# Casts of the gated heads held in order on ScalarE, their projection one gate later, and eight conv taps moved to an earlier product, in a hybrid mixer block

## The chip, the cores and the metric

The kernel runs on one core of one Trainium2 chip. Its time is the device time of one execution in microseconds (us). The kernel before takes 981.49 us, the median of three runs (981.21 to 982.88).

The core's engines each take instructions from a queue of their own, in order, and wait on semaphores for one another: TensorE (PE: matmuls, with its weight loads shown as PEld), VectorE (DVE), ScalarE (ACT), GpSimd (POOL) and SyncE (SP), which here only issues transfers.

## The reference

One layer on x of 512 positions by 1024 channels. Its first part, which the change touches, is cut to this:

```python
hn = rms_norm(h, g_mix_pre)
z_sgu, z_conv, z_pool, z_gate = split(hn @ w_in)         # 2048, 2048, 1024, 3072 columns
# A: spatial gating
u, v = split(gelu(z_sgu))
v = layer_norm(v, g_v, b_v)                              # in 4 blocks of 128 positions, 8 heads of 128 channels
mixed = einsum('hij,bnjhc->bnihc', masked(w_s), v) + b_s
br_a = (u * mixed) @ w_sgu_out
# B: conformer convolution
a, gate = split(z_conv)
c = causal_depthwise_conv(a * sigmoid(gate), w_dw) + b_dw # 31 taps in each channel
br_b = silu(layer_norm(c, g_ln, b_ln)) @ w_conv_out
# C: pooling: trailing means over 2, 4, 8, 16 positions in 4 groups of 256 channels, minus z
br_c = (einsum('bsgc,gcd->bsgd', trailing_means(z_pool) - z_pool, w_pool) * s_pool) @ w_pool_out
g = sigmoid(z_gate)                                      # three gates of 1024 channels
merged = g[0] * br_a + g[1] * br_b + g[2] * br_c
h = h + rms_norm(merged @ w_out, g_mix_post)
```

A SwiGLU part with 2816 channels and a gated embedding follow; the change leaves their code as it is.

## The kernel before

**Products.** Activations stand transposed, 128 channels by 512 positions a tile, 8 tiles. Every float32 operand is held as two parts in TensorE's float32r format: `hi`, the value cast, and `lo`, the rest. A product of two 128-blocks is three matmuls (`mm3`): hi by hi, hi by lo, lo by hi. An output tile of 128 channels from 1024 inputs is 24 matmuls. The weights of one such tile are one block `raw` of 128x1024, loaded by SP; ScalarE casts `hi<-raw` and VectorE subtracts `lo<-raw,hi`. Three buffers of each rotate, so a cast waits until TensorE has finished with an older block, and a load until VectorE has finished with an older `raw`.

**Stages around the change, in the program's order.** Conv input (`ps_ag`, a and gate of branch B). v's product (`ps_nat`, positions on the partitions; `natural`), gelu, and v's normalisation (`v_norm`, `v_gain`: rows `v_all`). u's product, also `ps_nat`. Between its pieces stand the heads: `mix_head(h)` splits v of head h (`v_split`), multiplies it by the head's 128x128 matrix (`ps_mix`), gates it with u (`gated`), turns its 32x32 blocks (`corners`) and sends it by way of DRAM (`home`) back into `sgu`, turned as a whole. `split_head(h)` then casts the head that has come back (ACT `sgu<-sgu`) and subtracts (DVE `sgu<-sgu`). Then the eight gate tiles of branch A (`ps_gate`, a sigmoid into `merged`) and the eight tiles of its projection (`ps_br<-sgu`), which start `SGU_LAG` gates behind. Then the pooling input (`ps_z`, copied to `z_all`): for each of four groups of two tiles, GpSimd adds up the windows (`win`), VectorE finishes them with three instructions on `win`, ScalarE casts `pl_hi<-win`, VectorE subtracts `pl_lo<-win,pl_hi`, and TensorE maps the group (`ps_pool`, 24 matmuls), called map 1 to 4 here. Then the gates of branch C with its projection (`ps_br<-pool`), branch B's norm, gates and projection, and the rest.

**Conv taps.** The 31 taps of each of the 8 conv tiles are VectorE work for which no other engine waits until branch B's norm: one `TENSOR_SCALAR` and thirty `SCALAR_TENSOR_TENSOR acc<-h_conv,vec,acc` a tile. They stand in the list `background`; `drain(n)` places n of them. `TAPS` says how many go behind each tile of the conv input, each weight block of v's product, each gate or projection tile of branch A, each tile of the pooling input, and each tile of branch C's gates and projection; `TAPS_U` does so for u's product.

**What sets the order.** The program is recorded in the order of the code, and a scheduler then places each engine's instructions by its own estimate of when their inputs are ready. Only where `order` is on (`InOrder`) does an instruction stay behind everything that was recorded before it on its engine. On before's ScalarE the casts of the heads are placed freely; `gated` and `corners` on VectorE and all conv taps are held.

Of the kernel before, what the change touches and what calls it, by code (L numbers as in the profile page):

```python
# [7 lines left out]
F32 = mybir.dt.float32  # L8
# [4 lines left out]
ALU = mybir.AluOpType  # L13
# [30 lines left out]

N_WARM = 8

TAPS = (4, 3, 5, 4, 5)
TAPS_U = 4


# [42 lines left out]
def hybrid_block(  # L93
# [8 lines left out]
    order = InOrder(tc)  # L102
    dve, act_e = order.engine(nc.vector), order.engine(nc.scalar)
# [21 lines left out]
    def t2(name, n=T):  # L125
        return tmp.tile([P, n], F32, tag="t2", name=name)
# [50 lines left out]
    def split(hi, lo, src):  # L177
        act_e.copy(hi, src)
        dve.tensor_tensor(out=lo, in0=src, in1=hi, op=ALU.subtract)
# [75 lines left out]
    def drain(n):  # L255
        for _ in range(min(n, len(background))):
            with order():
                background.pop(0)()
# [63 lines left out]
    def add_mix(*blocks):  # L322
        for b in blocks:
            weights.add(w_mix[b])
# [3 lines left out]
    add_mix(*range(C_V, C_V + 8))  # L328
    weights.add(w_sgu, "tm")
    add_mix(*range(C_U, C_U + 8))  # L330
    SGU_LAG = 5
    for n in range(KT + SGU_LAG):
        if n < KT:
            add_mix(C_M + n)
        if n >= SGU_LAG:
            add_mix(S_SGU + n - SGU_LAG)
    for g in GROUPS:
# [96 lines left out]
    def glu(k, ps_a, ps_g, scale=None):  # L434
        sig = t2("sig")
        src = ps_g
        if scale is not None:
            dve.tensor_tensor(out=sig, in0=ps_g, in1=scale, op=ALU.mult)
            src = sig
        act_e.activation(out=sig, in_=src, func=AF.Sigmoid)  # L440
        if scale is not None:
            dve.tensor_tensor(out=sig, in0=sig, in1=scale, op=ALU.mult)
        dve.tensor_tensor(out=h_of(k), in0=ps_a, in1=sig, op=ALU.mult)
        queue_conv(k)
# [14 lines left out]
    with order():  # L459
        (c0, c1), cut = first_cuts(0)  # L460
        hi, lo = (w[:, c0:c1] for w in first[0])
# [4 lines left out]
        hi, lo = (w[:, slice(*cut)] for w in first[0])  # L466
# [40 lines left out]
        for i in range(KT):  # L507
            t = t2("nrm")
            dve.scalar_tensor_tensor(out=t, in0=x_all[:, i], scalar=col("g_mix_pre", i),
                                     in1=x_inv, op0=ALU.mult, op1=ALU.mult)  # L510
            act_e.copy(hn[i][:, 0], t)
            if low:
                low()
            low = lambda i=i, t=t: dve.tensor_tensor(out=hn[i][:, 1], in0=t, in1=hn[i][:, 0],
                                                     op=ALU.subtract)
# [6 lines left out]
    for k in range(N_RAW, KT):  # L522
        pair = []
        for _ in range(2):
# [4 lines left out]
            pair.append(ps)  # L529
            drain(TAPS[0])  # L530
        glu(k, *pair)


    def natural(dst, evacuate, taps):


        for c in range(2):
            banks = [bank("ps_nat") for _ in range(NB)]
            for kk in range(4):
                hi, lo = weights.get()  # L540
                for b in range(NB):
                    if b == NB // 2:
                        yield c, kk, 0
                    ts = slice(b * P, (b + 1) * P)
                    for j in range(2):
                        k = 2 * kk + j
                        a = hn[k]
                        ws = slice(j * T, (j + 1) * T)
                        pe.matmul(banks[b], lhsT=a[:, 0, ts], rhs=hi[:, ws],
                                         start=k == 0, stop=False)  # L550
                        pe.matmul(banks[b], lhsT=a[:, 1, ts], rhs=hi[:, ws],
                                         start=False, stop=False)
                        pe.matmul(banks[b], lhsT=a[:, 0, ts], rhs=lo[:, ws],
                                         start=False, stop=k == KT - 1)
                drain(taps)
                if kk == 3:
                    for b in range(NB):
                        evacuate(dst, b, c, banks[b])
                yield c, kk, 1
# [23 lines left out]
    nc.sync.dma_start(out=b_bc, in_=gb_v[1:2, :].broadcast_to([P, D]))  # L583
    for _ in natural(v_all, v_gelu, TAPS[1]):
        pass
# [32 lines left out]
    def mix_head(h):  # L618
        cs = slice(h * P, (h + 1) * P)
        vs = slot("tm", "v_split")  # L620
        split(vs[:, 0], vs[:, 1], of_head(v_tile, h))
        ps = bank("ps_mix")
        mm3(ps, sg_hi[:, cs], sg_lo[:, cs], vs[:, 0], vs[:, 1], True, True)


        gated, corners = t2("gated"), t2("corners")
        sgu_T[h] = slot("br", f"sgu{h}")
        with order():
            dve.scalar_tensor_tensor(out=gated, in0=ps, scalar=col("b_sgu_s", h),
                                     in1=of_head(u_tile, h), op0=ALU.add, op1=ALU.mult)  # L630
            dve.transpose(out=corners, in_=gated)
        home = dram.tile([P, T], F32, name="home")
        for i in range(NQ):
            nc.sync.dma_start(
                out=home[:, i * P:(i + 1) * P].rearrange("(q a) f -> a q f", q=NQ),
                in_=corners[i * Q:(i + 1) * Q].rearrange("a (q f) -> a q f", q=NQ))
        nc.sync.dma_start(out=sgu_T[h][:, 1].bitcast(F32), in_=home)

    def split_head(h):
        hi, lo = sgu_T[h][:, 0], sgu_T[h][:, 1]  # L640
        split(hi, lo, lo.bitcast(F32))


    heads = {(1, 0): ((), (0,)), (1, 1): ((), (1,)), (2, 1): ((0,), (2,)),
             (3, 0): ((1,), ()), (3, 1): ((), (3,))}
    for c, kk, behind in natural(u_all, u_gelu, 0):
        pe_order.on = c == 1 or kk == 3
        done, mixed = heads.get((kk, behind), ((), ())) if c == 1 else ((), ())
        for h in done:
            split_head(h)  # L650
        for h in mixed:
            mix_head(h)
        if behind:
            drain(TAPS_U)
# [5 lines left out]
    def gate_tile(dst, taps, between=None):  # L660
        ps = bank("ps_gate")
        w = weights.get()
        half = KT // 2 if between else KT
        product(ps, w, hn[:half], last=not between)
        if between:
            between()
            product(ps, [h[:, half * P:] for h in w], hn[half:], k0=half)
        act_e.activation(out=dst, in_=ps, func=AF.Sigmoid)
        drain(taps)

    def branch_tile(acts, taps):
        ps = bank("ps_br")
        product(ps, weights.get(), acts)
        drain(taps)
        return ps

    for n in range(KT + SGU_LAG):
        if n < KT:
            gate_tile(merged[:, n, :], TAPS[2])
        if n < SGU_LAG:  # L680
            for h in ((2,), (3,), (4,), (5, 6), (7,))[n]:
                split_head(h)
            for h in ((4,), (5, 6), (7,), (), ())[n]:
                mix_head(h)
        else:
            i = n - SGU_LAG
            ps = branch_tile(sgu_T, TAPS[2])

            gate = merged[:, i, :].rearrange("p (n i b) -> p i n b", n=NB, i=NQ)
            dve.tensor_tensor(out=gate, in0=ps.rearrange("p (i n b) -> p i n b", n=NB, i=NQ),  # L690
                              in1=gate, op=ALU.mult)
# [6 lines left out]
    def pool_windows(gi):  # L698
        w = WINDOWS[gi]
        z = z_all[:, 2 * gi:2 * gi + 2, :]  # L700
        cur, d = z, 1
        while d < w:
            nxt = slot("tm", "win", F32)
            nc.gpsimd.tensor_tensor(out=nxt[:, :, d:], in0=cur[:, :, d:], in1=cur[:, :, :T - d], op=ALU.add)
            nc.gpsimd.tensor_copy(nxt[:, :, :d], cur[:, :, :d])
            cur, d = nxt, 2 * d
        head = rcnt[:, None, :w].broadcast_to([P, 2, w])
        dve.tensor_tensor(out=cur[:, :, :w], in0=cur[:, :, :w], in1=head, op=ALU.mult)
        dve.tensor_tensor(out=cur[:, :, :w], in0=cur[:, :, :w], in1=z[:, :, :w], op=ALU.subtract)
        dve.scalar_tensor_tensor(out=cur[:, :, w:], in0=cur[:, :, w:], scalar=1.0 / w,  # L710
                                       in1=z[:, :, w:], op0=ALU.mult, op1=ALU.subtract)
        hi = slot("tm", "pl_hi")
        lo = slot("tm", "pl_lo")
        split(hi, lo, cur)
        pooled[gi] = hi, lo
# [13 lines left out]
    for g in GROUPS:  # L729
        for n in (2 * g, 2 * g + 1):  # L730
            ps = bank("ps_z")
            product(ps, weights.get(), hn)
            act_e.copy(z_all[:, n, :], ps)
            drain(TAPS[3])
        pool_windows(g)
# [5 lines left out]
    for n in range(KT + POOL_LAG):  # L741
        if n < KT:
            gates.append(t2("gate"))
            gate_tile(gates[n], TAPS[4], maps.get(n))
        if n == KT + POOL_LAG - 1:
# [104 lines left out]
    with order():  # L850
# [6 lines left out]
        for i in range(N_HALF):  # L857
            n = KT - N_HALF + i
# [9 lines left out]
        for i in range(N_HALF):  # L868
            n = KT - N_HALF + i
# [232 lines left out]
```

## Time and profile before

| | |
|---|---|
| median of 3 runs | 981.49 us |
| profiled execution, its own time | 981.05 us |
| its span, first to last instruction | 979.1 us |
| PE busy | 967.0 us (99%) |
| DVE busy | 679.1 us (69%) |
| ACT busy | 349.0 us (36%) |
| POOL busy | 70.8 us (7%) |
| mean granted TensorE clock | 0.996 of full speed |

The span is what the trace holds; 1.95 us of the profiled execution's own time lie around it, and the median of the runs is 0.44 us above that execution. In a row of a timeline stand the start, the duration, the engine, the operation and its tiles (out<-in), and in brackets the engine's idle time just before it with what ended that. "xN" is a number of instructions that the row merges. A matmul's duration overlaps the next one's, so TensorE's pace is read from starts. In the waits stand the total, the number of times, and the longest.

### The profile page before, as it was taken

Reading aid. Unit: us, or ns where it says so; the run is one execution under the profiler, and the core shown is the slowest. Engines: PE = TensorE matmul, PEld = TensorE weight load, DVE = VectorE, ACT = ScalarE, POOL = GpSimd, SP = SyncE. Lnnn points to the kernel's source line nnn. Section 1 sums busy time; section 2 is a strip of 40 time slices with the busy share of each in tenths; the row PEclk is TensorE's granted clock in tenths of the full one; section 3 lists DMA queues with packets and bytes.
Section 4 is the critical chain, followed back from the end, with each engine's and each line's share of the span. In section 5 each row is a group of like instructions: output and inputs, shape, how many; then the busy total and the mean of one; then the engine's idle time right before and its main releaser. Section 6 shows DMA issues by size and latency. Waiting matters only on the chain.

```text
span 979.1 us, 11157 instructions
## 1 busy us (share of the span) xinstructions
PE 967.0 (99%) x4397; PEld 803.4 (82%) x4397; DVE 679.1 (69%) x876; ACT 349.0 (36%) x467; POOL 70.8 (7%) x49
## 2 busy tenths in 40 slices
PE   9999999999997999999999999999999999999998
PEld 6888888888886878888888998888888888888887
DVE  7987789989999899977655688454445442223684
ACT  7522324333223332246525443332323232223451
POOL 0100013000022712220000000000000000000000
PEclk9999999999998999999999999999999999999999
DMA  8723322553322233232337303223232223334311
GB/s 301 203 88 106 109 87 81 164 160 112 108 78 84 76 108 108 87 108 86 108 108 237 107 1 128 87 86 104 90 108 87 99 83 100 100 100 140 110 65 65
DMA packets 36484, 106.92 MB, mean 109 GB/s; under 512 B 4176, under 2 KB 8784, under 8 KB 36432
## 3 DMA queue, kind: packets, MB, share of 16 engines
q1 hardware_dynamic: 35568, 103.95, 32.0%
q0 software_dynamic: 720, 2.23, 1.3%
q8 instruction: 34, 0.56, 0.2%
q14 instruction: 18, 0.15, 0.0%
q10 hardware_dynamic: 144, 0.04, 0.0%
HBM read 99.78 MB, written 4.19 MB: 106 GB/s over the span
## 4 chain that ended last, share of the span: by engine, by line
PE 79%; DVE 15%; issue 3%; DMA 2%; ACT 0%; SPq 0%; DVEq 0%; ACTq 0%
PE ps_f L80 25%; PE ps_fo L80 12%; PE ps_br L80 9%; PE ps_gate L80 8%; DVE acc L80 8%; PE ps_ag L80 6%; PE ps_o L80 5%; PE ps_pg L80 4%; PE ps_nat L80 4%; DVE lo L80 4%; PE ps_first L80 3%; PE ps_ple L80 1%; DMA sgu<-home 1%; DVE v_all L80 1%; DMA home<-corners 1%
## 5 line engine op out<-in xcount | busy, mean ns | idle before, releaser
L80 ACT CAST hi<-raw 128x1024 fp32r<-128x1024 f32 (+2 forms) x160 | 164.8, 1031 | 420.6 <-PE ps_br L80 85.4
L80 DVE TENSOR_TENSOR lo<-raw,hi 128x1024 fp32r<-128x1024 f32 (+2 forms) x158 | 205.6, 1302 | 104.6 <-ACT hi L80 103.8
L80 DVE SCALAR_TENSOR_TENSOR acc<-h_conv,vec,acc 128x509 f32<-128x509 f32 (+14 forms) x240 | 188.5, 790 | 4.3
L80 PE MATMUL ps_f<-hg,hi 128*128 128x512 f32 (+1 forms) x608 | 183.3, 383 | 0.0
L80 PEld LDWEIGHTS ps_f<-hg,hi 128*128 128x128 f32 x608 | 113.1, 188 | 22.5
L80 PE MATMUL ps_gate<-hn,hi 128*128 128x512 f32 x384 | 119.0, 389 | 0.0
L80 PE MATMUL ps_f<-hg,lo 128*128 128x512 f32 (+1 forms) x304 | 116.4, 383 | 0.0
L80 PE MATMUL ps_fo<-f,hi 128*128 128x512 f32 x352 | 108.4, 389 | 0.0
L80 PEld LDWEIGHTS ps_gate<-hn,hi 128*128 128x128 f32 x384 | 72.1, 188 | 15.0
L80 PE MATMUL ps_nat<-hi,hn 128*128 128x512 f32 x256 | 78.8, 389 | 0.0
L80 PEld LDWEIGHTS ps_fo<-f,hi 128*128 128x128 f32 x352 | 66.1, 188 | 13.6
L80 PE MATMUL ps_gate<-hn,lo 128*128 128x512 f32 x192 | 74.8, 390 | 1.2 <-DVE lo L80 1.2
L80 PE MATMUL ps_fo<-f,lo 128*128 128x512 f32 x176 | 68.5, 389 | 0.0
L80 PEld LDWEIGHTS ps_f<-hg,lo 128*128 128x128 f32 x304 | 57.1, 188 | 11.1
L80 DVE TENSOR_TENSOR f<-ps_f,h_inv 128x512 f32<-128x512 f32 x22 | 15.2, 690 | 59.4 <-PE ps_f L80 59.4
L80 PEld LDWEIGHTS ps_nat<-hi,hn 128*128 128x128 f32 x256 | 48.1, 188 | 9.9
L80 PE MATMUL ps_nat<-lo,hn 128*128 128x512 f32 x128 | 49.8, 389 | 0.0
L80 PE MATMUL ps_ag<-hn,hi 128*128 128x512 f32 x160 | 49.3, 389 | 0.0
L80 PEld LDWEIGHTS ps_gate<-hn,lo 128*128 128x128 f32 x192 | 36.0, 188 | 9.2 <-DVE lo L80 1.7
L80 PE MATMUL ps_z<-hn,hi 128*128 128x512 f32 x128 | 41.6, 406 | 0.0
L80 DVE TENSOR_TENSOR silu<-ps_f,h_inv 128x512 f32<-128x512 f32 x22 | 15.2, 690 | 36.7 <-PE ps_f L80 36.6
L80 PE MATMUL ps_br<-sgu,hi 128*128 128x512 f32 x128 | 39.4, 389 | 0.0
(220 smaller groups left out, 1488.6 us busy)
## 6 DMA issues: line engine op xcount, KB each, us to landing
raw<-in_w_mix SPq DMA_DIRECT2D x90, 512.0 KB, 3.2
raw<-in_w_ffn_in SPq DMA_DIRECT2D x44, 512.0 KB, 3.2
raw<-in_w_ffn_out SPq DMA_DIRECT2D x16, 448.0 KB, 3.3
raw<-in_w_ffn_out SPq DMA_DIRECT2D x8, 512.0 KB, 3.5
raw<-in_w_ple_gate SPq DMA_DIRECT2D x8, 512.0 KB, 3.5
x_all<-in_xT SPq DMA_DIRECT2D x8, 256.0 KB, 6.0
home<-corners SPq DMA_DIRECT2D x32, 64.0 KB, 2.6
sgu<-home SPq DMA_DIRECT2D x8, 256.0 KB, 2.6
```

The lines of the kernel that those rows point to most:

```text
L80: inst = op(*args, **kw)
```

## The change

The casts of the eight returned heads (`act_e.copy(hi, ...)` in `split_head`) are recorded under `order`, so that each stays behind all that was recorded before it on ScalarE; the calls are placed later (heads 0 and 1 in the fourth weight block of u's second half, heads 2 to 7 one gate later than before), and the projection starts six gates behind (`SGU_LAG`), with the order of its weight blocks changed to match. Behind each of the eight weight blocks of v's product stand four conv taps where there were three, and behind each of the eight tiles of the pooling input three where there were four.

```diff
-TAPS = (4, 3, 5, 4, 5)
+TAPS = (4, 4, 5, 3, 5)
...
-    SGU_LAG = 5
+    SGU_LAG = 6
...
     def split_head(h):
         hi, lo = sgu_T[h][:, 0], sgu_T[h][:, 1]
-        split(hi, lo, lo.bitcast(F32))
+        with order():
+            act_e.copy(hi, lo.bitcast(F32))
+        dve.tensor_tensor(out=lo, in0=lo.bitcast(F32), in1=hi, op=ALU.subtract)
...
-    heads = {(1, 0): ((), (0,)), (1, 1): ((), (1,)), (2, 1): ((0,), (2,)),
-             (3, 0): ((1,), ()), (3, 1): ((), (3,))}
+    heads = {(1, 0): ((), (0,)), (1, 1): ((), (1,)), (2, 1): ((), (2,)),
+             (3, 0): ((0,), ()), (3, 1): ((1,), (3,))}
...
-            for h in ((2,), (3,), (4,), (5, 6), (7,))[n]:
+            for h in ((), (2,), (3,), (4,), (5, 6), (7,))[n]:
                 split_head(h)
-            for h in ((4,), (5, 6), (7,), (), ())[n]:
+            for h in ((4,), (5, 6), (7,), (), (), ())[n]:
                 mix_head(h)
```

The order that the scheduler makes of it differs on every engine from v's product to branch C's gates, with the same instructions in all. Three places follow.

ScalarE, from just ahead of head 0's cast, before; `sgu_` with a number is one returned head's tile, the lowest number is head 0:

```order
L80 CAST v_split<-v_all 128x512
L80 CAST sgu_1350<-sgu_1350 128x512
L80 CAST hi<-raw 128x1024
L80 CAST v_split<-v_all 128x512
L80 ACTIVATE u_all<-ps_nat 128x16x32
L80 CAST sgu_1380<-sgu_1380 128x512
L80 ACTIVATE u_all<-ps_nat 128x16x32 x2
L80 CAST hi<-raw 128x1024
L80 ACTIVATE u_all<-ps_nat 128x16x32
L80 CAST v_split<-v_all 128x512
L80 CAST sgu_1434<-sgu_1434 128x512
L80 CAST hi<-raw 128x1024
```

ScalarE now, again from just ahead of head 0's cast, to the first gate's sigmoid (`merged`):

```order
L80 CAST hi<-raw 128x1024
L80 CAST sgu_1358<-sgu_1358 128x512
L80 CAST v_split<-v_all 128x512
L80 ACTIVATE u_all<-ps_nat 128x16x32 x3
L80 CAST hi<-raw 128x1024
L80 ACTIVATE u_all<-ps_nat 128x16x32
L80 CAST sgu_1388<-sgu_1388 128x512
L80 CAST v_split<-v_all 128x512
L80 CAST hi<-raw 128x1024
L80 ACT_TABLE_LOAD
L80 ACTIVATE merged<-ps_gate 128x512
```

Heads 0 and 1 are cast one weight block (`hi<-raw`) later than before; head 2, which stands in the first list, is beyond the end of the second, two blocks later and behind two sigmoids.

VectorE, from the subtraction of a map's weights to the last window row of map 2 (`win<-win,z_all 128x2x4`), before; `acc` rows are conv taps:

```order
L80 TENSOR_TENSOR lo<-raw,hi 128x512
L80 SCALAR_TENSOR_TENSOR acc_154<-h_conv_150,vec,acc_154 128x488
L80 SCALAR_TENSOR_TENSOR pool_2373<-ps_pool,vec,pool_2373 128x512
L80 SCALAR_TENSOR_TENSOR win<-win,z_all 128x2x508
L80 TENSOR_TENSOR win<-win,rcnt 128x2x4
L80 SCALAR_TENSOR_TENSOR acc_154<-h_conv_150,vec,acc_154 128x487
L80 TENSOR_TENSOR lo<-raw,hi 128x1024
L80 TENSOR_TENSOR win<-win,z_all 128x2x4
```

The same stretch of VectorE now:

```order
L80 TENSOR_TENSOR lo<-raw,hi 128x512
L80 SCALAR_TENSOR_TENSOR acc_154<-h_conv_150,vec,acc_154 128x484
L80 SCALAR_TENSOR_TENSOR win<-win,z_all 128x2x508
L80 TENSOR_TENSOR win<-win,rcnt 128x2x4
L80 SCALAR_TENSOR_TENSOR pool_2377<-ps_pool,vec,pool_2377 128x512
L80 SCALAR_TENSOR_TENSOR acc_154<-h_conv_150,vec,acc_154 128x483
L80 TENSOR_TENSOR win<-win,z_all 128x2x4
```

The 128x1024 weight subtraction has moved behind the last window row, and the tap at the same place is four taps further in its tile (483 elements left where 487 were).

TensorE at map 4, the difference from before to now (the first two matmuls of the map take `pl_hi`, its other ten begin with `pl_lo`):

```order
+L80 MATMUL ps_pool<-pl_hi,hi 128x512 x2
 L80 MATMUL ps_gate<-hn_160,hi 128x512 x2
 L80 MATMUL ps_gate<-hn_160,lo 128x512
-L80 MATMUL ps_gate<-hn_161,hi 128x512
-L80 MATMUL ps_pool<-pl_hi,hi 128x512 x2
-L80 MATMUL ps_gate<-hn_161,hi 128x512
-L80 MATMUL ps_gate<-hn_161,lo 128x512
-L80 MATMUL ps_gate<-hn_162,hi 128x512 x2
-L80 MATMUL ps_gate<-hn_162,lo 128x512
-L80 MATMUL ps_gate<-hn_163,hi 128x512
 L80 MATMUL ps_pool<-pl_lo,hi 128x512
```

The first two matmuls of map 4 stand four matmuls earlier in TensorE's queue, and the other ten follow three matmuls behind them instead of six.

## The prediction

> **What bounds the kernel now.** I read the page first, then TensorE's waits, then its timeline at each of them, and last the queue of the engine it waited for.
>
> ```profile
> PE 967.0 (99%) x4397; PEld 803.4 (82%) x4397; DVE 679.1 (69%) x876; ACT 349.0 (36%) x467; POOL 70.8 (7%) x49
> PE   9999999999997999999999999999999999999998
> PEclk9999999999998999999999999999999999999999
> ```
>
> TensorE is busy 99% of the span. The one dip, in busy time and in granted clock, lies in the slice from 294 to 318 us: the pooling input. The change removes no matmul, so it can only win back what TensorE loses by waiting:
>
> ```profile
> PE ps_pool L80 <- ACT pl_hi L80: 5.5, 2, 3.1
> PE ps_gate L80 <- DVE lo L80: 1.2, 1, 1.2
> PE ps_br L80 <- DVE lo L80: 0.4, 1, 0.4
> ```
>
> TensorE's timeline at the waits of maps 1 and 2 and of the gate, and its pace in a stretch without waits:
>
> ```profile
> 294.77 0.39 PE L80 MATMUL ps_z<-hn,lo 128*128 128x512 f32 x1
> 297.58 0.73 PE L80 MATMUL ps_pool<-pl_hi,hi 128*128 128x512 f32 x2 [2.42 <-ACT pl_hi L80]
> ...
> 302.49 0.40 PE L80 MATMUL ps_pool<-pl_lo,hi 128*128 128x512 f32 x1
> ...
> 312.71 0.39 PE L80 MATMUL ps_z<-hn,lo 128*128 128x512 f32 x1
> 316.20 1.22 PE L80 MATMUL ps_pool<-pl_hi,hi 128*128 128x512 f32 x2 [3.10 <-ACT pl_hi L80]
> ...
> 319.68 0.63 PE L80 MATMUL ps_z<-hn,hi 128*128 128x512 f32 x2
> ...
> 345.24 0.61 PE L80 MATMUL ps_gate<-hn,hi 128*128 128x512 f32 x2
> 347.09 0.50 PE L80 MATMUL ps_gate<-hn,lo 128*128 128x512 f32 x1 [1.23 <-DVE lo L80]
> ...
> 376.87 5.44 PE ps_gate L80 x24
> ```
>
> The pace is 5.44/24 = 0.227 us a matmul. At map 1 the next matmul was due at 295.00 and came at 297.58: 2.58 us. The 14 matmuls from there to 302.49 took 4.91 us where 3.17 is the pace: 1.74 more. Map 2: due 312.94, came at 316.20, 3.26 us; then 8 matmuls in 3.48 instead of 1.81, 1.67 more. The gate: due 345.69, came at 347.09, 1.40. With the 0.4 at the projection (`ps_br`), TensorE loses 4.3 + 4.9 + 1.4 + 0.4 = 11.0 us. The slow matmuls behind the two long waits are a lower clock:
>
> ```profile
> 290.00:316.00 26.00, 20.68 (x83) 16.27 (x81) 25.64 (x34) 7.88 (x11) 6.26 (x4) 0.93 0.26 90
> 316.00:330.00 14.00, 13.80 (x54) 11.31 (x55) 11.10 (x11) 4.90 (x8) 9.68 (x7) 0.88 0.20 60
> ```
>
> (Length, busy time of PE, PEld, DVE, ACT, POOL, then the clock.) 0.07 of 26 us is 1.8, 0.12 of 14 is 1.7: the two excesses. Behind the gate's 1.2 us no such excess shows. The Trainium skill, "TensorE: Matmul & The Clock Gate", section "Why this matters for your kernels", allows gaps of up to about 3 us before the clock falls. Here a gap of 2.42 us was followed by the slow clock, so the measurement decides: a leftover wait like map 1's is priced at 4.3, where the page would make it 2.6.
>
> Who is late? The chain for a map is GpSimd's window sums, VectorE's three `win` rows, ScalarE's `pl_hi` cast:
>
> ```profile
> 287.55 1.18 POOL L705 COPY win<-z_all 128x2 f32<-128x2 f32 x1
> 294.39 1.21 DVE L80 SCALAR_TENSOR_TENSOR win<-win,z_all 128x1020 f32<-128x1020 f32 x1
> 296.24 0.15 DVE L80 TENSOR_TENSOR win<-win,z_all 128x4 f32<-128x4 f32 x1
> 296.49 1.05 ACT L80 CAST pl_hi<-win 128x1024 fp32r<-128x1024 f32 x1 [5.42 <-DVE win L80]
> ...
> 304.75 0.63 POOL L705 COPY win<-win 128x4 f32<-128x4 f32 x1
> 311.88 1.20 DVE L80 SCALAR_TENSOR_TENSOR win<-win,z_all 128x1016 f32<-128x1016 f32 x1
> 315.10 1.04 ACT L80 CAST pl_hi<-win 128x1024 fp32r<-128x1024 f32 x1 [6.09 <-DVE win L80]
> ```
>
> GpSimd had finished at 288.73 and 305.38; VectorE came to its first `win` row 5.7 and 6.5 us later, with no idle time before it. VectorE's queue is the bound from v's product to the maps, and conv taps are most of it. From v's normalisation to map 2 it idled only here:
>
> ```profile
> DVE sgu L80 <- ACT sgu L80: 5.9, 4, 2.2
> ACT sgu L80 <- DMA sgu<-home: 33.3, 8, 10.3
> 169.87 1.06 ACT L80 CAST hi<-raw 128x1024 fp32r<-128x1024 f32 x1 [1.87 <-PE ps_nat L80]
> 181.75 0.62 ACT L80 CAST sgu<-sgu 128x512 fp32r<-128x512 f32 x1 [10.30 <-DMA sgu<-home]
> 182.28 1.05 ACT L80 CAST hi<-raw 128x1024 fp32r<-128x1024 f32 x1
> 182.41 0.69 DVE L80 TENSOR_TENSOR sgu<-sgu 128x512 fp32r<-128x512 f32 x1 [2.19 <-ACT sgu L80]
> 218.18 0.61 PE L80 MATMUL ps_br<-sgu,hi 128*128 128x512 f32 x2
> 221.20 0.62 ACT L80 CAST sgu<-sgu 128x512 fp32r<-128x512 f32 x1 [3.16 <-DMA sgu<-home]
> 221.85 0.69 DVE L80 TENSOR_TENSOR sgu<-sgu 128x512 fp32r<-128x512 f32 x1 [0.52 <-ACT sgu L80]
> ```
>
> All eight casts stood waiting for their head's transfer, and four times VectorE waited with them: 5.9 us of a queue that is late.
>
> **The change, part by part.** *Eight taps into v's product.* VectorE's room there, and its price of a tap and of a weight subtraction:
>
> ```profile
> 94.00:137.00 43.00, 43.00 (x191) 35.64 (x190) 33.37 (x45) 14.71 (x19) 1.29 (x1) 1.00 0.33 111
> 224.25 3.85 DVE L80 SCALAR_TENSOR_TENSOR acc<-h_conv,vec,acc 128x505 f32<-128x505 f32 x5
> 228.02 1.22 DVE L80 TENSOR_TENSOR lo<-raw,hi 128x1024 fp32r<-128x1024 f32 x1
> ```
>
> A tap takes 0.75 us behind another and about 0.65 between other rows. Eight are 5.2 to 6.0 us; 43.0 - 33.4 = 9.6 us are free. They cost nothing, hidden by VectorE's waits for the next weight cast; if that cover were gone, v's normalisation would start up to 6 us late, and `v_split`, `ps_mix` and TensorE behind it.
>
> *Eight fewer in the pooling input.* Counted in the order from v's first normalising row to the last `win` row of each map, the taps fall from 108, 119, 127, 134 to 106, 115, 120, 127: at 0.7, 1.4, 2.8, 4.9 and 4.9 us less ahead of maps 1 to 4. Ahead of map 2's last row a weight subtraction (1.1 us) and, ahead of its first, a `pool` row (0.65) have moved behind as well; the second is back before the last row.
>
> *Casts later.* Head 0 landed at 181.7 and its slot is now behind the weight cast that before ran at 182.28 after that very wait (TensorE frees that block's buffer near 176, an estimate: 169.87, one block of 5.44 and one head's three matmuls). ScalarE still stands until 181.7, with a `v_split`, three gelus of u and a weight cast behind it; VectorE wants the first of these at about 185.5. VectorE now has two more taps and a weight subtraction ahead of that head, 2.5 us, so it gets there near 183.6 instead of 180.2: the 2.19 us wait goes. The other seven casts waited 33.3 - 10.3 = 23.0 us in all before, 3.3 each; their heads are turned no later now, and the casts stand one tile of 5.44 us or two later, most behind a gate's sigmoid (the last one ends at 218.2), so the heads are there. I take all 5.9 us as gone; ends: 0 and 5.9, nearer the latter since only the first head's slot comes close to its landing.
>
> *Projection one gate later.* TensorE reaches it 5.44 us later, with a gate in between, so no matmul time changes. The last head's rest (VectorE, 221.85 before) comes after 8 more taps and two more weight subtractions, 8.2 us, less the 5.9: 224.2. TensorE needs it at 218.2 + 5.4 + 7 × 0.68 = 228.4. Its 0.4 us wait goes. SP now issues one load ahead of head 6's return; GpSimd adds one conv tile ahead of map 3's windows (up to 1.3 us); both lie in margins of over 2 us.
>
> *The maps.* VectorE would reach map 1's last `win` row at 296.2 - 1.4 - 5.9 = 288.9; GpSimd's end holds it to 288.7 + 2.1 = 290.8. TensorE wants the cast done by 294.6: no wait, 2.8 us to spare. From there to map 2's first `win` row VectorE took 15.5 us; two taps and one `pool` row fewer make it 13.4, so 304.2, last row 306.8, cast done 308.0. TensorE, no longer stopped, arrives at 312.9 - 4.3 - 0.4 = 308.2. That is a margin of 0.2 us. Map 3 is bounded by GpSimd and has about 3. Map 4's `pl_lo` stands seven matmuls earlier in TensorE's queue:
>
> ```profile
> 332.96 0.16 DVE L80 TENSOR_TENSOR win<-win,z_all 128x16 f32<-128x16 f32 x1
> 352.52 0.17 DVE L80 TENSOR_TENSOR win<-win,z_all 128x32 f32<-128x32 f32 x1
> 357.67 0.39 PE L80 MATMUL ps_pool<-pl_lo,hi 128*128 128x512 f32 x1
> ```
>
> It is wanted at 357.7 - 11.0 - 1.6 = 345.1. VectorE took 19.6 us from map 3's last `win` row to map 4's, with the same rows in between now, and 2.6 more to the end of `pl_lo`; map 3's last row comes at 322.2 by the walk (an estimate; GpSimd's sums bound it), so 344.4. The gate's wait for `lo` goes too: VectorE is 10 us earlier there, TensorE 9.6. So two places are tight, each with an error of about 1 us either way; half of such cases wait, 0.7 us on average, too short for the slow clock. I take 0.7 for both together; ends 0 and 4.3 (map 1's price).
>
> **Sum.** 11.0 - 0.7 = 10.3 us. Against the profiled execution (981.05, 1.95 of it outside the span) 970.8; against the median, 0.44 above it, 971.2.
>
> **Rivals.** *A long wait stays.* If VectorE wins back only part of the 5.9 us, or GpSimd's sums stretch, map 2 or 4 stops TensorE for 2.5 us and the clock falls: 971.2 + 4.3 + about 0.5 = 976. For it: the margins of 0.2 us, and that VectorE is held up while GpSimd adds windows, here three taps in 5.41 us where 2.2 is usual:
>
> ```profile
> 299.93 5.41 DVE L80 SCALAR_TENSOR_TENSOR acc<-h_conv,vec,acc 128x495 f32<-128x495 f32 x3
> ```
>
> Against it: every map but these two has over 2 us. *No change.* The waits move from `pl_hi` to weight `lo` rows in the same tiles, since the taps' sum up to branch C is the same: 981. Against it: the order has the map's rows and the weight subtractions earlier together. *Slower.* Pinned behind sigmoids, the casts come when TensorE ends a gate, and VectorE, whose subtractions are in order too, idles a tile of 5.4 us for one of them beyond today's 5.9. From 7.3 us of idle on (5.9 and the 1.4 of two taps) map 1 gets its cast later than now; at 11.3 it and the earlier `pl_lo` of map 4 stop TensorE 4 us longer: 985.5. Against it: by the walk each cast is ready 1.5 to 6 us before VectorE comes to it.
>
> **How the numbers follow.** Forecast (0 to 2.5 us left waiting, 970.3 to 973) 0.68; a long wait stays, 0.19; no change 0.05; slower 0.08. 0.2% of the time, 2.0 us, is about what a measurement of this kernel can tell from no change. Faster: 0.68 + 0.19 = 0.87; same 0.05; slower 0.08. The range goes from 970.0, all 11.0 us won and a little for the runs' scatter, to 977.0, where one long wait is left.
>
> **What would show it.** Right: no wait of TensorE for `pl_hi` over 1 us, no slice below 9 in PEclk, no DVE wait for ACT `sgu`, the first `win` row of map 1 right behind GpSimd's end, 8 more taps ahead of `v_all`. Wrong: TensorE waiting at `ps_mix` (the taps did not fit), at `ps_br<-sgu` (the heads are late), or still at maps 2 or 4 with clock below 1.

## The result, and the profile after

The changed kernel takes 970.85 us (median of 4 runs, 970.82 to 971.22) against 981.92 us for the kernel before beside it: ratio 0.9887, 95% interval 0.987 to 0.9905. The forecast was 971.2. The profiled execution has a span of 968.9 us; before it was 979.1. The medians lie 11.1 us apart and the profiled executions 10.2, since that of the kernel before was 0.9 us below its median here.

The page's busy row, TensorE's slices and its granted clock after the change, and then all of TensorE's waits of 0.1 us and over but those of the first microseconds (engine, tile, releaser: us in total, times, longest):

```profile
PE 963.0 (99%) x4397; PEld 801.4 (83%) x4397; DVE 681.3 (70%) x876; ACT 349.5 (36%) x467; POOL 74.2 (8%) x49
PEclk9999999999999999999999999999999999999999
```

```profile
PE ps_pool L80 <- ACT pl_hi L80: 0.9, 1, 0.9
```

The two long waits at the maps, the gate's and the projection's are gone, and with the long waits the slices of low clock. TensorE's own busy time fell from 967.0 to 963.0: the prediction counted 1.74 + 1.67 us for matmuls at a lower clock, which is 3.4 of those 4 us. One wait of 0.9 us is left, at map 2.

The heads' casts on ScalarE, and the first head's rest on VectorE:

```profile
182.28 0.62 ACT L80 CAST sgu<-sgu 128x512 fp32r<-128x512 f32 x1 [5.08 <-DMA sgu<-home]
187.51 0.62 ACT L80 CAST sgu<-sgu 128x512 fp32r<-128x512 f32 x1 [1.17 <-DMA sgu<-home]
184.04 0.68 DVE L80 TENSOR_TENSOR sgu<-sgu 128x512 fp32r<-128x512 f32 x1
```

ScalarE waits for two transfers (6.3 us) where it waited for eight (33.3 us), and VectorE for no cast at all (5.9 us before).

Maps 1 and 2, over GpSimd, VectorE, ScalarE and TensorE:

```profile
286.60 0.64 POOL L707 COPY win<-z_all 128x2 f32<-128x2 f32 x1
289.89 1.22 DVE L80 SCALAR_TENSOR_TENSOR win<-win,z_all 128x1020 f32<-128x1020 f32 x1
291.74 0.16 DVE L80 TENSOR_TENSOR win<-win,z_all 128x4 f32<-128x4 f32 x1
291.99 1.05 ACT L80 CAST pl_hi<-win 128x1024 fp32r<-128x1024 f32 x1 [1.42 <-DVE win L80]
294.50 0.62 PE L80 MATMUL ps_pool<-pl_hi,hi 128*128 128x512 f32 x2
...
307.84 0.16 DVE L80 TENSOR_TENSOR win<-win,z_all 128x8 f32<-128x8 f32 x1
308.09 1.04 ACT L80 CAST pl_hi<-win 128x1024 fp32r<-128x1024 f32 x1 [3.92 <-DVE win L80]
309.19 0.73 PE L80 MATMUL ps_pool<-pl_hi,hi 128*128 128x512 f32 x2 [0.93 <-ACT pl_hi L80]
```

At map 1 the cast is done at 293.04, 1.5 us before TensorE comes. But VectorE's first `win` row starts 2.65 us after GpSimd's end (287.24): VectorE is still late there, only less.

### The profile page after: what moved, and what is told of

The parts are those of the page before. It is cut to its first block, busy times and chain, and to the rows that moved or that the text cites. A ratio compares the mean times of both kernels' runs of the same rounds, so it can differ in the third digit from the quotient of the medians.

```text
span 968.9 us, 11159 instructions
## 1 busy us (share of the span) xinstructions
PE 963.0 (99%) x4397; PEld 801.4 (83%) x4397; DVE 681.3 (70%) x876; ACT 349.5 (36%) x467; POOL 74.2 (8%) x49
## 4 chain that ended last, share of the span: by engine, by line
PE 98%; DVE 1%; issue 0%; ACT 0%; DVEq 0%; ACTq 0%
PE ps_f L80 25%; PE ps_gate L80 13%; PE ps_br L80 13%; PE ps_fo L80 12%; PE ps_nat L80 9%; PE ps_ag L80 6%; PE ps_o L80 5%; PE ps_pg L80 5%; PE ps_z L80 4%; PE ps_first L80 3%; PE ps_ple L80 1%; PE ps_pool L80 1%; PE ps_mix L80 1%; PE ps_warm L80 0%; PE ps_stat L80 0%; DVE lo L80 0%
## 5 line engine op out<-in xcount | busy, mean ns | idle before, releaser
L80 DVE TENSOR_TENSOR lo<-raw,hi 128x1024 fp32r<-128x1024 f32 (+2 forms) x158 | 213.7, 1353 | 101.2 <-ACT hi L80 100.8
L80 DVE SCALAR_TENSOR_TENSOR acc<-h_conv,vec,acc 128x511 f32<-128x511 f32 (+17 forms) x240 | 183.4, 768 | 4.5
L80 PEld LDWEIGHTS ps_f<-hg,lo 128*128 128x128 f32 x304 | 57.1, 188 | 11.1
L80 PE MATMUL ps_z<-hn,hi 128*128 128x512 f32 x128 | 39.6, 389 | 0.0
L80 PE MATMUL ps_br<-pool,hi 128*128 128x512 f32 x128 | 39.5, 389 | 0.0
```

The lines of the kernel that those rows point to most:

```text
L80: inst = op(*args, **kw)
```

## The experiments

Theory Q, that of the prediction: TensorE lost its 11 us because VectorE's queue came late to the maps, and it was late for two reasons, its idle time at the heads and the conv taps ahead of the maps. Rivals: the taps alone do it (T), the casts alone do it (C). All runs below were timed against the kernel before on the same chip, whose median was 981.65 to 982.21 us.

| Kernel | us, median (range) | ratio, 95% interval | TensorE waits at `pl_hi`: us in total, longest | VectorE waits at `sgu`, us |
|---|---|---|---|---|
| taps only | 977.0 (976.61 to 977.37) | 0.9956 (0.9941 to 0.997) | 2.9, 2.5 | 6.2 |
| casts only | 973.79 (973.48 to 973.93) | 0.9922 (0.9906 to 0.9938) | 1.5, 1.5 | none |
| casts not held | 977.04 (976.79 to 977.82) | 0.9958 (0.9943 to 0.9973) | 3.9, 3.2 | 5.7 |
| held, early places | 976.42 (975.91 to 977.81) | 0.9944 (0.9931 to 0.9958) | 4.1, 3.3 | 3.1 |
| lag of five | 972.09 (971.65 to 973.04) | 0.9907 (0.9888 to 0.9925) | 2.0, 2.0 | 0.4 |
| no conv sums | 969.97 (969.63 to 970.69) | 0.9881 (0.9867 to 0.9894) | none | none |
| bias added on VectorE | 975.56 (974.87 to 976.31) | 0.9937 (0.9924 to 0.9949) | 3.0, 3.0 | none |
| ten more taps | 970.18 (969.93 to 970.82) | 0.9883 (0.9869 to 0.9896) | none | none |
| sixteen more taps | 981.89 (981.18 to 982.9) | 1.0009 (1.0 to 1.0018) | none | none |

**The taps alone.**

```diff
-TAPS = (4, 3, 5, 4, 5)
+TAPS = (4, 4, 5, 3, 5)     # kernel before otherwise
```

> Only the table of taps is changed, (4, 4, 5, 3, 5); heads, casts and the projection's lag are as in the kernel before. Theory Q (VectorE's late queue at the maps, made of idle time at the heads and of taps ahead): the casts stand early again, VectorE idles about 5 us at them, map 1's last win row comes only 1 to 2 us earlier than before and map 2's about 4.5 us earlier, so TensorE still waits about 1.2 us at map 1 and 2 us at map 2: 973.5 to 976 us. Rival T (the eight taps alone suffice): no wait for pl_hi over 1 us, 971 us. Rival C (taps do nothing, the casts do it all): 981 us.

Measured 977.0: T and C fall, and Q's 973.5 to 976 is missed by 1 us. VectorE's waits, TensorE's, and map 1's first `win` row:

```profile
DVE sgu L80 <- ACT sgu L80: 6.2, 5, 2.2
PE ps_pool L80 <- ACT pl_hi L80: 2.9, 2, 2.5
PE ps_gate L80 <- DVE lo L80: 0.6, 1, 0.6
296.55 1.21 DVE L80 SCALAR_TENSOR_TENSOR win<-win,z_all 128x1020 f32<-128x1020 f32 x1
```

With two taps fewer ahead of it, map 1 is not earlier than before the change (294.39) but 2.2 us later. Of this 0.5 us was there from the start (v's product begins at 93.59 instead of 93.06, v's normalisation at 142.06 instead of 141.52). The stretch from the normalisation to the end of map 1's last `win` row is 1.6 us longer, 156.5 us instead of 154.9. VectorE idles 0.3 us more at the heads, and two things that Q had not priced are in the rest: rows stretched beside GpSimd's work, which lose 12.9 us in all where they lost 11.9, and taps that follow one of their own tile where before they alternated between two. Both come back below. The wait at the gate is a head's too, by way of VectorE's order:

```profile
222.54 0.62 ACT L80 CAST sgu<-sgu 128x512 fp32r<-128x512 f32 x1 [3.29 <-DMA sgu<-home]
223.06 1.05 ACT L80 CAST hi<-raw 128x1024 fp32r<-128x1024 f32 x1
223.19 0.69 DVE L80 TENSOR_TENSOR sgu<-sgu 128x512 fp32r<-128x512 f32 x1 [1.80 <-ACT sgu L80]
224.45 1.22 DVE L80 TENSOR_TENSOR lo<-raw,hi 128x1024 fp32r<-128x1024 f32 x1
225.72 0.50 PE L80 MATMUL ps_gate<-hn,lo 128*128 128x512 f32 x1 [0.59 <-DVE lo L80]
```

VectorE stood 1.80 us for the head's cast. The weight's subtraction, one tap behind the head's in its order, began at 224.45, 0.34 us after its `hi` cast was done (224.11), and reached TensorE 0.6 us late.

**The casts alone.**

```diff
-TAPS = (4, 4, 5, 3, 5)
+TAPS = (4, 3, 5, 4, 5)     # changed kernel otherwise
```

> The held casts, their later places and the lag of 6 are kept, and the taps are put back to (4, 3, 5, 4, 5). Theory Q: no VectorE wait for a sgu cast; map 1 just in time (two more taps use up the 1.5 us it has in the changed kernel); map 2's last win row comes some 2.8 us later than in the changed kernel, TensorE waits 3 to 4 us there and the granted clock falls once: 974 to 976 us. Rival C (the casts do it all): 971 us. Rival T (the taps do it all): 981 us.

Measured 973.79, just below Q's range, and T and C are both out: the casts are worth 8 us alone, the taps 4.8 alone, and together 11, less than the sum; by the prediction's count 11 us was all that TensorE lost. Q's wait at map 2 was too long: 1.46 us came where 3 to 4 were expected, and its clock stayed at 1.00. TensorE's waits at the maps, and map 1's last `win` row:

```profile
PE ps_pool L80 <- ACT pl_hi L80: 1.5, 1, 1.5
PE ps_pool L80 <- DVE pl_lo L80: 0.6, 1, 0.6
291.62 0.16 DVE L80 TENSOR_TENSOR win<-win,z_all 128x4 f32<-128x4 f32 x1
```

Two taps more stand ahead of map 1 than in the changed kernel, and yet VectorE takes 149.3 us from v's normalisation (142.49) to the end of this row, where the changed kernel takes 150.2. Rows beside GpSimd's work lose 12.1 us in that stretch instead of 13.1, and 13 taps follow one of another tile instead of 2, worth 1.3 us (see "Map 1" below); the two taps cost some 1.4. From there to map 2's last row it takes 17.5 us instead of 16.1, with two taps more, and there TensorE waits.

**Which half of the casts' change does it: the hold or the place?** With the new taps in all, four kernels fill the square; neither is the kernel of the taps alone (977.0) and both is the changed kernel (970.85). The place without the hold:

```diff
-        with order():
-            act_e.copy(hi, lo.bitcast(F32))
-        dve.tensor_tensor(out=lo, in0=lo.bitcast(F32), in1=hi, op=ALU.subtract)
+        split(hi, lo, lo.bitcast(F32))
```

> The changed kernel with the casts of the turned heads no longer held in the written order on ScalarE; taps, later places and the lag of 6 stay. The scheduler then puts the heads' rests into VectorE's queue at the same counts of taps as in the kernel with only the taps changed. Theory Q: VectorE idles about 5 us at the heads again, and the time is that of the taps alone, 973.5 to 976 us, within 0.5 us of it. Rival P (the later place and the longer lag do it, the hold on ScalarE does nothing): 971 us, no VectorE wait for sgu over 0.5 us.

Measured 977.04, the same as the taps alone and like it 1 us above Q's range, with the casts waiting for their transfers and VectorE for them as before:

```profile
ACT sgu L80 <- DMA sgu<-home: 34.2, 8, 10.7
DVE sgu L80 <- ACT sgu L80: 5.7, 4, 2.2
```

So the later place in the code does nothing by itself: the scheduler moves the unheld cast forward again, and all eight stand behind the same weight casts as with the taps alone. The hold without the place:

```diff
-    SGU_LAG = 6
+    SGU_LAG = 5      # and both lists of heads as in the kernel before; casts held
```

> Taps as in the changed kernel, the casts held in the written order on ScalarE, but heads and projection in their early places (as in the kernel before). This fills the last corner: hold without the later place. Theory Q (both are needed: the hold keeps a cast where it is written, the later place lets the transfer land first): ScalarE stands at each head with weight casts queued behind it, VectorE idles 3 to 6 us at the heads, 974 to 979 us. Rival H (the hold alone is enough, because VectorE's own row is held back as well): VectorE idles under 1.5 us, 971 to 972.5 us.

Measured 976.42: held at the early place, a cast still stands before its head has landed. ScalarE waits 29.9 us for seven transfers, VectorE 3.1 us for the casts, TensorE 4.1 us for `pl_hi`. Rival H falls. Only hold and place together let most of the transfers land first.

**The lag.**

```diff
-    SGU_LAG = 6
+    SGU_LAG = 5      # the last six heads one gate earlier; casts held, first two heads late
```

> The changed kernel with the projection one gate earlier again (lag 5) and the last six heads one gate earlier; the casts stay held, the taps stay (4, 4, 5, 3, 5). Map 2 then has one tap and one weight subtraction more ahead of its last win row. Theory Q: the heads' casts wait for their transfers for part of the time, VectorE idles 0 to 2 us at them; map 2 1.8 to 3.8 us later than in the changed kernel, so a TensorE wait of 2.5 to 4.5 us there, with slow clock behind: 973 to 976 us; the projection itself waits under 0.5 us. Rival L (the lag buys nothing): 971 us. Rival M (the projection comes too early for the last head): a TensorE wait of over 1 us at ps_br, 972 to 975 us with no wait at map 2.

Measured 972.09. Rival M falls (no wait at `ps_br`). Against rival L stands the trace more than the time, which is 0.9 to 1.2 us above the changed kernel's two medians (971.17 and 970.85), with ranges that overlap for one of them. Q had the place right and the size too large: TensorE waits 2.04 us at map 2, where the changed kernel waits 0.93, and no slow clock follows. This kernel differs from the one just above (976.42) only in the later places of the first two heads: those are worth 4.3 us, the later places of the other six and the lag about 1.

**What GpSimd's additions cost VectorE.** Map 1 came later in the changed kernel than a count of its rows says. Here GpSimd's running sum of conv tiles 2 to 6 is left out:

```diff
-        elif k > 1:
+        elif k == 7:
             nc.gpsimd.tensor_tensor(out=conv_sum, in0=conv_sum, in1=acc_of(k), op=ALU.add)
```

> The changed kernel without GpSimd's additions of conv tiles 2 to 6 to the running sum (that part of the result is left out); VectorE's and TensorE's rows and their order are unchanged. Theory G (VectorE's two-input rows are stretched while GpSimd adds): the rows beside those additions lose 0.8 to 1.1 us each, three of them ahead of map 1; its first win row comes about 2.5 us earlier, map 2's last win row 2 to 3 us earlier, the wait of 0.9 us goes: 969.6 to 970.2 us. Rival R (rows have the length they have): map 1 within 0.5 us of the changed kernel, 0.9 us wait stays, 970.9 us.

VectorE's order is the same to the row. The changed kernel's second addition on GpSimd, the four taps beside it, and the same four taps in this kernel:

```profile
233.73 2.60 POOL L426 TENSOR_TENSOR conv_sum<-conv_sum,acc 128x512 f32<-128x512 f32 x1 [34.64 <-DVE acc L80]
235.09 4.13 DVE L80 SCALAR_TENSOR_TENSOR acc<-h_conv,vec,acc 128x511 f32<-128x511 f32 x4
```

```profile
234.38 3.10 DVE L80 SCALAR_TENSOR_TENSOR acc<-h_conv,vec,acc 128x511 f32<-128x511 f32 x4
288.72 1.22 DVE L80 SCALAR_TENSOR_TENSOR win<-win,z_all 128x1020 f32<-128x1020 f32 x1
306.54 0.16 DVE L80 TENSOR_TENSOR win<-win,z_all 128x8 f32<-128x8 f32 x1
```

One addition costs these taps 1.03 us. Theory G holds: the wait at map 2 is gone and the time is 969.97. Its size at the maps was half of what was expected: both come 1.2 to 1.3 us earlier, not 2 to 3, since VectorE gave some of it back by idling 1.1 us on the way to map 1.

**The bias on VectorE.** The largest stretches are four rows beside GpSimd's additions of v's bias.

```diff
-        nc.gpsimd.tensor_tensor(out=v_all[:, b], in0=v_all[:, b], in1=grouped(b_bc), op=ALU.add)
+        dve.tensor_tensor(out=v_all[:, b], in0=v_all[:, b], in1=grouped(b_bc), op=ALU.add)
```

> The changed kernel with the four additions of v's bias (128x1024, fp32) on VectorE in place of GpSimd. Theory G: four VectorE rows that now take 2.9 to 3.4 us fall to 1.2 (about 8.7 us less in all) and four rows of 1.2 us come (4.6 us), so VectorE is about 4 us earlier from there; map 1 is then bounded by GpSimd's window sums, map 2 has no TensorE wait: 969.6 to 970.3 us. Rival R (nothing is stretched by GpSimd): VectorE 4.6 us later, TensorE stops at maps 1 and 2 as before the change: 975 to 979 us.

The changed kernel's addition and the subtraction beside it, and then that subtraction in this kernel:

```profile
143.90 2.85 POOL L601 TENSOR_TENSOR v_all<-v_all,b_bc 128x1024 f32<-128x1024 f32 x1 [8.95 <-DVE v_all L80]
144.41 3.43 DVE L80 TENSOR_TENSOR lo<-raw,hi 128x1024 fp32r<-128x1024 f32 x1
```

```profile
144.79 1.22 DVE L80 TENSOR_TENSOR lo<-raw,hi 128x1024 fp32r<-128x1024 f32 x1
```

The mechanism is as G said, 3.43 us against 1.22, and the time is not: 975.56, where G had 970 and R, whose mechanism is refuted by these rows, 975 to 979. VectorE's waits from v's normalisation to map 1, where the changed kernel has none, and TensorE's:

```profile
DVE merged L80 <- PE ps_br L80: 2.0, 3, 0.8
DVE lo L80 <- ACT hi L80: 1.6, 4, 0.5
DVE gated L80 <- PE ps_mix L80: 1.4, 4, 0.6
```

```profile
PE ps_pool L80 <- ACT pl_hi L80: 3.0, 1, 3.0
```

VectorE was early, and its order is fixed, so it spent most of what it had won on 5.0 us of waits for TensorE and ScalarE ahead of map 1: that stretch took 149.2 us, 1.0 less than in the changed kernel. That order is also another one: the scheduler, with other rows to place, put 12 taps and three 128x1024 weight subtractions between maps 1 and 2 where the changed kernel has 9 and two, some 3.4 us more at 0.73 and 1.2 us, and 19.1 us lie between the two last `win` rows instead of 16.1. So map 2 became the late place. An early engine wins nothing when the rows ahead of the next due place grow.

**How much v's product can hide.**

```diff
-TAPS = (4, 4, 5, 3, 5)
+TAPS = (5, 4, 5, 2, 5)     # and, for sixteen, (4, 6, 5, 1, 5)
```

> The changed kernel with taps (5, 4, 5, 2, 5): ten more ahead of v's normalisation (80 instead of 70), five fewer between it and map 2. Theory Q: ten taps are some 7 us and v's product has 5.2 us left (43.0 - 37.8), so the normalisation starts about 1.8 us later; map 2's last win row comes some 1.8 us earlier, the 0.9 us wait goes, ps_mix does not wait: 969.7 to 970.3 us. Rival V (no cover left): a TensorE wait of 1 us or more at ps_mix or the v split, 971.5 to 973 us. Rival N (map 2 was not the last loss that counts): 970.9 us as the changed kernel.

> Taps (4, 6, 5, 1, 5): 16 more than the changed kernel ahead of v's normalisation (86), 3 fewer from there to map 1 and 10 fewer to map 2. Sixteen taps are about 11.5 us, of which v's product hides 5.2 at most. Theory Q (the cover is gone): the normalisation starts 6 to 7 us later than in the changed kernel, VectorE comes 2 to 4 us later to map 1, TensorE waits 1 to 4 us at ps_mix or map 1, and if over 2.2 us in one piece the clock falls: 972 to 976 us. Rival F (VectorE catches up, since only map 2 and the maps behind it are tight): no wait over 0.5 us, 970.2 us.

The ten stand behind the tiles of the conv input, the sixteen in v's product. VectorE in v's product in the changed kernel, with ten more taps and with sixteen more (window, its length, then busy time of PE, PEld, DVE, ACT, POOL, clock):

```profile
94.00:137.00 43.00, 43.00 (x192) 35.59 (x191) 37.76 (x53) 14.71 (x19) 2.86 (x1) 1.00 0.33 111
```

```profile
94.00:137.00 43.00, 43.00 (x192) 35.61 (x191) 40.04 (x54) 14.88 (x18) 1.53 (x1) 1.00 0.33 110
```

```profile
94.00:137.00 43.00, 43.00 (x191) 35.60 (x190) 40.17 (x54) 14.92 (x18) 1.72 (x1) 1.00 0.34 109
```

In these kernels it does not get above 40.2 of 43 us. The prediction's "free" time was not all free: once VectorE does 40 of 43, further taps push v's normalisation back, from 141.69 to 144.84 with ten more and to 151.72 with sixteen; 0.5 us of each is a later start of v's product itself, so the taps cost 2.7 and 9.5 us:

```profile
144.84 1.53 DVE L80 TENSOR_SCALAR v_all<-v_all,v_mv,v_y 128x1024 f32<-128x1024 f32 x2
```

```profile
151.72 1.53 DVE L80 TENSOR_SCALAR v_all<-v_all,v_mv,v_y 128x1024 f32<-128x1024 f32 x2
PE ps_mix L80 <- DVE v_split L80: 4.4, 1, 4.4
PE ps_mix L80 <- ACT v_split L80: 4.2, 1, 4.2
```

With ten more, nothing downstream notices: TensorE has no wait left but that for its first operands, and the time is 970.18, as Q had it. With sixteen, TensorE stands 8.6 us at `ps_mix`, and the whole gain is gone: 981.89, beyond Q's 972 to 976. Behind the second of these waits the clock is down, as the stretch from there shows:

```profile
176.70:190.70 14.00, 13.97 (x53) 11.43 (x54) 11.80 (x17) 4.66 (x7) 1.30 (x1) 0.85 0.36 115
```

The prediction had named this cover, and put its loss at up to 6 us for eight taps; sixteen pushed the normalisation back by 9.5 us, 0.60 us a tap.

The kernel with ten more taps and the changed kernel lie close, so both were run again side by side:

> The changed kernel once more, so that it stands beside the next run on the same chip at the same time. Every theory: 970.6 to 971.3 us.

> The kernel with ten more taps ahead of v's normalisation once more, beside the changed kernel. Theory Q (the 0.9 us wait at map 2 was TensorE's last loss there): 0.5 to 1.0 us less than the changed kernel. Rival N (no difference, the first look was scatter): within 0.3 us of it.

The changed kernel took 971.17 us (970.82 to 972.17; ratio 0.9899, 0.9886 to 0.9913), with the same 0.93 us wait at map 2; ten more taps took 970.35 (970.18 to 970.48; ratio 0.989, 0.9874 to 0.9905). The difference is 0.8 us, the size of that wait, and their ranges do not touch, though the intervals against the kernel before overlap. The kernel with ten more taps is the fastest of those that do the whole work, by less than 0.1%.

## Why the prediction was right

**The loss of 11.0 us, and that it was all there was to win.** Shown: with every wait of TensorE at the gates and maps gone, the time is 970.2 to 970.4, some 11.3 to 12 below the kernel before.

**Eight taps at no cost.** Right. v's normalisation started at 141.52 before and at 141.69 after, as much later as v's product itself (93.06 and 93.22). But the reason given, 9.6 us of free time, overstates it, as the two kernels with more taps show.

**The 5.9 us at the heads gone.** Right, to the last cast: first head's rest at 184.0 (forecast 183.6), the last one's at 224.7 (224.2), no wait at `ps_br`. The square of hold and place shows why: both are needed.

**Map 1.** Here a step failed. The prediction had VectorE 7.3 us earlier and so held by GpSimd's end, with the last `win` row at 290.8. VectorE came 4.5 us earlier (294.39 to 289.89), GpSimd held nothing, and the last row was at 291.74; the sign that the prediction named, the first `win` row right behind GpSimd's end, did not come. The failing term is "two taps fewer, 1.4 us". VectorE's taps between v's normalisation and map 1, before and after (busy us, mean ns, idle us):

```profile
L80 DVE SCALAR_TENSOR_TENSOR acc<-h_conv,vec,acc 128x511 f32<-128x511 f32 (+18 forms) x105 | 78.8, 760 | 1.5
```

```profile
L80 DVE SCALAR_TENSOR_TENSOR acc<-h_conv,vec,acc 128x504 f32<-128x504 f32 (+15 forms) x104 | 80.3, 773 | 1.9
```

With the first rows of tiles (4 before, 3 after, 0.54 us each) that is 109 taps in 81.0 us and 107 in 81.9 (each view takes in one tap that ends at its edge, so 108 and 106 by the prediction's count): fewer, and 0.9 us longer, with 0.4 us more idle between them. The 26 subtractions took 0.5 us more, the heads' subtractions 0.7 less. So the stretch went from 154.87 to 150.20 us, 4.7 shorter, not 7.3.

The two traces show where the missing 2.6 us went. First, rows beside GpSimd's additions and window sums took 11.9 us more than the usual step of their kind before, and 13.1 after: 1.2 us. That such additions cost VectorE time is shown by the kernel without three of them, which gave back 1.2 us at map 1 and 1.1 us of idle time. Second, a tap costs less behind a tap of another tile than behind one of its own. Three taps in a row before, and two after:

```profile
239.80 0.72 DVE L80 SCALAR_TENSOR_TENSOR acc<-h_conv,vec,acc 128x490 f32<-128x490 f32 x1
240.44 0.74 DVE L80 SCALAR_TENSOR_TENSOR acc<-h_conv,vec,acc 128x511 f32<-128x511 f32 x1
241.10 0.72 DVE L80 SCALAR_TENSOR_TENSOR acc<-h_conv,vec,acc 128x489 f32<-128x489 f32 x1
```

```profile
251.03 0.73 DVE L80 SCALAR_TENSOR_TENSOR acc<-h_conv,vec,acc 128x497 f32<-128x497 f32 x1
251.79 0.73 DVE L80 SCALAR_TENSOR_TENSOR acc<-h_conv,vec,acc 128x496 f32<-128x496 f32 x1
```

Before, two tiles alternate here (490, 511, 489 elements left), and the taps start 0.65 us apart. After, they run on in one tile, 0.77 apart on average. In the stretch to map 1, 13 pairs of taps are of the first kind before and 2 after: 11 times 0.12 us, 1.3 us. No run changed the order of the taps alone, so this second part rests on the rows of these traces. The prediction had seen the first cost (three taps in 5.41 us) and weighed it only as a rival at the maps, not as a term ahead of them; of the second it had both prices (0.75 and about 0.65) and took 0.7 for every tap.

**Map 2.** The walk from map 1's last row to map 2's was right (16.1 us, forecast 16.0), and it carried map 1's 0.9 us along. The cast, forecast for 308.0, was done at 309.13; TensorE came at 308.26 (forecast 308.2) and waited 0.93. The two tight places were given 0.7 together and one of them took 0.9; map 4's `pl_lo` came 0.3 us in time. A term wrong by 2.6 us thus made map 1 only 0.9 us later than forecast, because GpSimd's end was to hold VectorE there anyway, and it cost TensorE nothing at map 1, which had 2.8 us to spare. That 0.7 and 0.9 lie so close is luck: by the walk alone map 2 had 0.2 us to spare, the 0.7 stood for errors of either sign, and the wait that came is the 0.9 us of map 1.

**Sum.** 10.3 us was the forecast, and the span is 10.2 us shorter; the medians are 11.1 apart.

**Rivals.** None happened here. A long wait at map 2 with slow clock, the second likeliest, came in the kernel with the casts held at their early places and in that with the bias on VectorE: 3.3 and 3.0 us there, and 976.4 and 975.6 us, near the 976 that the rival was given.

## What to carry over

A cast that waits for a transfer holds up everything behind it on its engine; look for the next use that can bear it later, and hold it there in the order, since one without the other did next to nothing here (977.0 for neither or for the place alone, 976.4 for the hold alone, 970.9 for both). Price rows moved on VectorE with GpSimd's additions beside them and by the row ahead of them, not by the mean of a row, and look at the next due place after the one that was relieved. Idle time of an engine that feeds a critical one is not free to its full size: here 8 taps cost nothing, 18 delayed their engine by 2.7 us without harm, and 24 undid the whole gain.

## What the runs showed of the hardware

**A gap of TensorE is cheap up to about 2 us and dear from 2.4.** Behind gaps of 0.93, 1.46 and 2.04 us the granted clock in the next 14 us was 1.00; behind 2.45 and 2.96 us it was 0.88 (1.7 us lost), behind 3.22 (the casts not held) 0.89, behind 3.30 it was 0.78. Rows of the lag of five (2.04), the taps alone (2.45) and the casts held early (3.30):

```profile
311.00:325.00 14.00, 13.80 (x61) 11.44 (x62) 11.44 (x11) 5.00 (x9) 10.26 (x7) 1.00 0.26 91
```

```profile
299.00:313.00 14.00, 13.27 (x51) 10.81 (x52) 13.89 (x16) 5.54 (x8) 6.23 (x4) 0.88 0.29 87
```

```profile
313.00:327.00 14.00, 13.61 (x48) 11.00 (x49) 8.73 (x7) 5.09 (x8) 9.43 (x7) 0.78 0.19 55
```

The prediction had the step between 1.23 and 2.42 us; these runs put it between 2.04 and 2.42, by one gap of each length. The casts alone and the lag of five came out 0.2 and 0.9 us below the ranges expected of them: their waits were shorter than expected, and stayed below the step. The Trainium skill, "TensorE: Matmul & The Clock Gate", section "Why this matters for your kernels", puts the limit at about 3 us; the measurements here are lower.

**Rows of VectorE stand still while GpSimd adds.** The subtraction at 144.41 ended at 147.84, 1.09 us after GpSimd's addition ended (146.75), and a subtraction by itself takes 1.22: it seems to have begun only then. The Trainium skill, "SBUF — State Buffer", section "Who interferes with whom", says that a VectorE instruction with two inputs in SBUF and a GpSimd instruction that reads SBUF exclude each other, the later one blocking until the first is done; these two rows agree with it. By the trace's starts it is not always the later one that is held: in the changed kernel the running sum's addition that began at 233.73 took 2.60 us (1.30 at 197.79), while a subtraction of VectorE that began at 233.96 took its usual 1.22. And a row with one tile as its input was held up too: v's normalising row took 0.81 us at 141.69, and 2.89 beside the second addition of the bias:

```profile
150.75 2.89 DVE L80 TENSOR_SCALAR v_all<-v_all,v_mv,v_y 128x1024 f32<-128x1024 f32 x1
```
